# Seven products of matrix quarters instead of eight in part of a two-layer decoder trunk

## Chip, cores and metric

The kernel runs on one core of a Trainium2 chip. The metric is the device time of one execution in microseconds. Five engines work side by side, each through its own list of instructions in order, and wait for each other through semaphores: TensorE (PE in the profile; its loads of stationary operands are listed apart as PEld), VectorE (DVE), ScalarE (ACT), GpSimd (POOL) and SyncE (SP), which here issues the DMAs. SBUF has 128 partitions; TensorE writes into PSUM, whose tiles in this kernel have 512 or 2 x 512 fp32 values in a partition.

## The reference

Two layers on 512 tokens of width 1024, in fp32. Each layer adds a mixer and a SwiGLU feed-forward to the residual, each behind an RMSNorm; a last RMSNorm ends it.

```
h = x
h += sgu(rmsnorm(h, mix_g0));   h += swiglu(rmsnorm(h, ffn_g0))    # layer 0
h += ret(rmsnorm(h, mix_g1));   h += swiglu(rmsnorm(h, ffn_g1))    # layer 1
out = rmsnorm(h, fin_g)

sgu(n):  u, v = split(gelu(n @ w_in));  v = layernorm(v)            # 1024 -> 2 x 1024
         (u * (causal(w_s) @ v + b_s, per chunk of 128)) @ w_out    # 1024 -> 1024
ret(n):  q, k, v, g = split(n @ w_in)    # 4 heads: 256, 256, 512, 512 columns each
         q, k = rotary(q), rotary(k)/16; o = (q k^T * decay) v      # causal
         (rmsnorm(o per head) * gn_g * silu(g)) @ w_out             # 2048 -> 1024
swiglu(n): a, b = split(n @ w_gu);  (silu(a) * b) @ w_down          # hidden 2816
```

Counted in blocks of 1024 rows by 1024 columns of weights the projections are 27.5: `sgu_w_in` 2, `sgu_w_out` 1, two times gate/up 5.5 and down 2.75, `ret_w_in` 6, `ret_w_out` 2.

## The kernel before

Products keep fp32 precision in this way: each operand is split into a high part of the type fp32r and a low part, the rest, and three matmuls are added in PSUM: high by high, high by low, low by high. The weights are split on the chip: a DMA brings a raw tile of 256 rows by 512 columns (`wr`), ScalarE copies it to the high part (`wh`, L112), VectorE subtracts (`wl`, L113); with a gain for each row the lines are L116 and L117. `wr`, `wh` and `wl` have a tag of their own with three buffers each.

`project_t` (L136) makes four tiles of 128 output features by 512 tokens: stationary is a 128 x 128 piece of weights, moving are the 512 tokens of the input, transposed (features on the partitions). `project_n` (L164) makes four tiles of 128 tokens by 512 features: stationary are 128 tokens, moving are the weights. Both walk down the rows of the weights in pairs of 128 (`kp`), and for each of the four output tiles issue 2 x 3 matmuls: L148 to L150, or L159 to L161.

The residual lies transposed in eight tiles `xt`: features on the partitions, tokens along. `residual` (L251) adds the product to it from PSUM, splits the sum with the gain of the next norm into `XH` and `XL` (L238, L239) and adds its square to a running sum. The factor of RMSNorm, `R`, is not needed for the product: `norm_rows` (L208) sums the squares over the partitions with two matmuls against ones and takes the inverse root by three steps of Newton's, and the scaling by `R` is done on the product behind PSUM (L517 and L521 in gate/up, on the rotary tables and on v and g in the heads).

The order: input and its transposition, v in two halves, u in two halves with the mixing between, the gating output `so`; gate/up in eleven groups of 128 + 128 paired columns with silu, product and split behind each; down in two halves of 512 columns with 22 row tiles each; four heads with q and k (256 + 256 columns), v, the scores, g, the score-value product in transposed form, the norm of the head by `norm_rows` and the split of the result `z`; the retention output `ro` in two halves; gate/up again, in whose third and fourth group the residual is transposed back by 32 transposes (`xN`, L670); and down by tokens, its last tile cut in two pieces of 256 columns, so that the end of the kernel is short.

PSUM is held as seven tiles of one bank for products and one for small uses. Most other intermediate tiles (`B`) share one pool of 51. The order on each engine is made when the program is built: a planner walks the instructions by their place in the program as priority, puts each on its engine when its inputs and its tile are there by the planner's own times, and fixes that order; on the chip each engine then goes through its list.

Of the kernel before, what the change touches and what calls it, by code (L numbers as in the profile page):

```python
# [24 lines left out]
WAKE = 5  # L25
EPS = 1e-6
# [17 lines left out]

@with_exitstack
def trunk(ctx, tc, x, positions, mix_g, ffn_g, fin_g, sgu_w_in, sgu_w_s, sgu_b_s, sgu_ln_g, sgu_ln_b,
# [4 lines left out]
    big = ctx.enter_context(tc.tile_pool(name="big", bufs=51))  # L51
    wpool = ctx.enter_context(tc.tile_pool(name="wpool", bufs=3))
    tmp = ctx.enter_context(tc.tile_pool(name="tmp", bufs=6))
    small = ctx.enter_context(tc.tile_pool(name="small", bufs=4))
    psp = ctx.enter_context(tc.tile_pool(name="psp", bufs=7, space=PSUM))
    nps = ctx.enter_context(tc.tile_pool(name="nps", bufs=1, space=PSUM))

    def B(name, dtype=F32R, width=T):
        return big.tile([P, width], dtype, tag="b", name=name)
# [4 lines left out]
    def PS(name):  # L64
        return psp.tile([P, T], F32, tag="ps", name=name)

    def f32(t):
        return t.bitcast(F32)

# [4 lines left out]

    onesr = const.tile([P, P], F32R, name="onesr")
    nc.vector.tensor_copy(onesr, ones)

    nc.scalar.activation(const.tile([P, 1], F32, name="first"), ones[:, 0:1], AF.Gelu_apprx_tanh)
    wake = nps.tile([P, T], F32, tag="nps", name="wake")
    for _ in range(WAKE):  # L80
        nc.tensor.matmul(wake[:, 0:P], ones, ones, start=True, stop=True)
# [12 lines left out]
    def rows_to_cols(name):  # L94
        n = rows_in[name].shape[0]
        ps = nps.tile([P, T], F32, tag="nps", name=f"{name}_ps")
        nc.tensor.transpose(ps[:, 0:n], rows_in[name], ident[0:n, 0:n])
        cols = const.tile([P, n], F32, name=f"{name}_cols")
        nc.vector.tensor_copy(cols, ps[:, 0:n])
        return lambda m: cols[:, m:m + 1]  # L100

    def load_weights(load, name):
        wr = wpool.tile([P, 2, T], F32, tag="wr", name=f"wr_{name}")
        load(wr)
        return wr

    def split_weights(wr, name, cols=None):
        """Rows of the weights, times a gain for each if there is one, as the sum of two F32R parts."""
        wh = wpool.tile([P, 2, T], F32R, tag="wh", name=f"wh_{name}")
        wl = wpool.tile([P, 2, T], F32R, tag="wl", name=f"wl_{name}")  # L110
        if cols is None:
            nc.scalar.activation(wh, wr, AF.Copy)  # L112
            nc.vector.tensor_tensor(wl, wr, f32(wh), ALU.subtract)  # L113
        else:
            for a in range(2):
                nc.scalar.activation(wh[:, a, :], wr[:, a, :], AF.Copy, scale=cols[a])  # L116
                nc.vector.scalar_tensor_tensor(wl[:, a, :], wr[:, a, :], cols[a], f32(wh[:, a, :]), ALU.mult, ALU.subtract)  # L117
        return wh, wl

    def gain_pair(col_of, kp):  # L120
        return None if col_of is None else [col_of(2 * kp + a) for a in range(2)]

    def one_slice(w, c0):
        def load_at(kp):
            src = w[kp * 2 * P:(kp + 1) * 2 * P, c0:c0 + T].rearrange("(a p) n -> p a n", p=P)
            return lambda wr: nc.sync.dma_start(wr, src)
        return load_at

    def two_slices(w, c0, c1):
        def load_at(kp):  # L130
            def load(wr):
                for i, c in enumerate((c0, c1)):
                    src = w[kp * 2 * P:(kp + 1) * 2 * P, c:c + T // 2].rearrange("(a p) n -> p a n", p=P)
                    nc.sync.dma_start(wr[:, :, i * (T // 2):(i + 1) * (T // 2)], src)
            return load
        return load_at  # L136

    def project_t(name, load_at, kt, xh, xl, col_of=None):
        """Four tiles [128 output features, 512 tokens]."""
        ps = [PS(f"ps_{name}_{m}") for m in range(4)]  # L140
        for kp in range(kt // 2):
            n = f"{name}_{kp}"
            wh, wl = split_weights(load_weights(load_at(kp), n), n, gain_pair(col_of, kp))
            for m in range(4):
                for a in range(2):
                    k = 2 * kp + a
                    sl = slice(m * P, (m + 1) * P)
                    nc.tensor.matmul(ps[m], wh[:, a, sl], xh[k], start=(k == 0), stop=False)  # L148
                    nc.tensor.matmul(ps[m], wh[:, a, sl], xl[k], start=False, stop=False)  # L149
                    nc.tensor.matmul(ps[m], wl[:, a, sl], xh[k], start=False, stop=(k == kt - 1))  # L150
        return ps

    def natural_step(ps, c, kp, w, kt, xh, xl, n0=0, n1=T):
        wh, wl = w
        o = ps[:, 0:n1 - n0]
        for a in range(2):
            k = 2 * kp + a
            sl = slice(c * P, (c + 1) * P)
            nc.tensor.matmul(o, xh[k][:, sl], wh[:, a, n0:n1], start=(k == 0), stop=False)  # L159
            nc.tensor.matmul(o, xl[k][:, sl], wh[:, a, n0:n1], start=False, stop=False)  # L160
            nc.tensor.matmul(o, xh[k][:, sl], wl[:, a, n0:n1], start=False, stop=(k == kt - 1))  # L161

    def project_n(name, load_at, kt, xh, xl, col_of=None):
        """Four tiles [128 tokens, 512 output features]."""  # L164
        ps = [PS(f"ps_{name}_{c}") for c in range(NC)]
        for kp in range(kt // 2):
            n = f"{name}_{kp}"
            w = split_weights(load_weights(load_at(kp), n), n, gain_pair(col_of, kp))
            for c in range(NC):
                natural_step(ps[c], c, kp, w, kt, xh, xl)  # L170
        return ps

    def rsqrt_cols(src, n, scale, name):
        """(src * scale + EPS) ** -0.5 of [128, n]."""
        a = small.tile([P, n], F32, tag="ra", name=f"ra_{name}")
        nc.vector.tensor_scalar(a, src, scale, EPS, ALU.mult, ALU.add)
        return rsqrt_of(a, n, name)

    def rsqrt_of(a, n, name):
        i = small.tile([P, n], I32, tag="ri", name=f"ri_{name}")  # L180
        nc.vector.tensor_scalar(i, a.bitcast(I32), 1, None, ALU.logical_shift_right)
        y = small.tile([P, n], F32, tag="ry", name=f"ry_{name}")
        nc.vector.tensor_scalar(y.bitcast(I32), i, -1.0, float(0x5F3759DF), ALU.mult, ALU.add)
        for s in range(3):
# [4 lines left out]
            z = small.tile([P, n], F32, tag="ry", name=f"ry_{name}_{s}")  # L189
# [4 lines left out]
    def rows_of(cols, dst, name):  # L194
        """dst[p, 128 c + t] = cols[t, c] for all p."""
# [4 lines left out]
        ps = nps.tile([P, T], F32, tag="nps", name=f"rp_{name}")  # L200
        for i, part in enumerate((ch, cl)):
# [3 lines left out]
            nc.tensor.matmul(ps, onesr, dg.rearrange("p c t -> p (c t)"), start=(i == 0), stop=(i == 1))  # L205
        nc.vector.tensor_copy(dst, ps)

    def norm_rows(acc, scale, R, name):  # L208
        """R[p, t] = (sum over the partitions of acc[:, t] * scale + EPS) ** -0.5 for all p."""
        h = tmp.tile([P, T], F32R, tag="t", name=f"nh_{name}")  # L210
        nc.scalar.activation(h, acc, AF.Copy)
        l = tmp.tile([P, T], F32R, tag="t", name=f"nl_{name}")
        nc.vector.tensor_tensor(l, acc, f32(h), ALU.subtract)
        ps = nps.tile([P, T], F32, tag="nps", name=f"ns_{name}")
        nc.tensor.matmul(ps, onesr, h, start=True, stop=False)
        nc.tensor.matmul(ps, onesr, l, start=False, stop=True)
        a = TMP(f"na_{name}")
        nc.vector.tensor_scalar(a, ps, scale, EPS, ALU.mult, ALU.add)
        nc.vector.tensor_scalar(R.bitcast(I32), a.bitcast(I32), 1, None, ALU.logical_shift_right)
        nc.vector.tensor_scalar(R.bitcast(I32), R.bitcast(I32), -1.0, float(0x5F3759DF), ALU.mult, ALU.add)  # L220
        t = TMP(f"nt_{name}")
        for _ in range(3):
            nc.vector.tensor_tensor(t, R, R, ALU.mult)
            nc.vector.scalar_tensor_tensor(t, t, -0.5, a, ALU.mult, ALU.mult)
            nc.vector.scalar_tensor_tensor(R, t, 1.5, R, ALU.add, ALU.mult)

    xt = [None] * KD
    XH = xpool.tile([P, KD, T], F32R, name="XH")
    XL = xpool.tile([P, KD, T], F32R, name="XL")
    xh = [XH[:, m, :] for m in range(KD)]  # L230
    xl = [XL[:, m, :] for m in range(KD)]
    acc = [None]

    def R_tile(name):
        return const.tile([P, T], F32, tag="R", name=f"R_{name}", bufs=2)

    def split_x(m, src, col):
        nc.scalar.activation(xh[m], src, AF.Copy, scale=col)  # L238
        nc.vector.scalar_tensor_tensor(xl[m], src, col, f32(xh[m]), ALU.mult, ALU.subtract)  # L239

    def add_square(m, src, name):
        sq = TMP(f"sq_{name}_{m}")
        nc.scalar.activation(sq, src, AF.Square)
        if m == 0:
            acc[0] = sq
        else:
            s = TMP(f"acc_{name}_{m}")
            nc.vector.tensor_tensor(s, acc[0], sq, ALU.add)
# [527 lines left out]
```

## Time and profile before

| | us |
|---|---|
| median of 3 runs (lowest, highest) | 1284.7 (1284.63, 1285.21) |
| span of the profiled execution | 1281.7 |
| busy: TensorE, VectorE, ScalarE | 1269.5, 686.7, 410.7 |

The span reaches from the first to the last instruction of one profiled execution; the time of the runs is that of the whole launch. Busy times of TensorE count overlapped matmuls once. A row of the timeline has the start in us, the duration, the engine, the line, the operation, the tiles (out<-in, numbers left out) and shapes, how many were merged, and in brackets the idle time before it and who ended it. A group row has count, busy time, mean duration in ns, idle time before and what ended it. A row of the waits has who waited for whom, us in total, how often, and the longest.

### The profile page before, as it was taken

The page shows a single profiled execution, that of the slowest core. Times are in us where ns is not written, and L with a number is a line of the kernel's source. Part 1 is how long each engine was busy: PE and PEld are TensorE (multiplying, and loading weights), DVE is VectorE, ACT ScalarE, POOL GpSimd, SP SyncE. Part 2 cuts the span into 40 slices and gives each one's busy share as a digit, 9 for nine tenths or more (in the row PEclk, how much of TensorE's full clock was granted, in tenths as well). Part 3 has the DMA queues.
Part 4 walks back from the last instruction along what each step waited for, and adds up shares of the span by engine and source line. Part 5 has one row for each costly group of instructions (what it writes and reads, how often), then busy time and mean ns, then how long its engine had stood idle before and what let it go on. Part 6 is the DMA issues. An engine that isn't in the chain of part 4 may idle for free.

```text
span 1281.7 us, 14479 instructions
## 1 busy us (share of the span) xinstructions
PE 1269.5 (99%) x5778; PEld 1057.3 (82%) x5778; DVE 686.7 (54%) x962; ACT 410.7 (32%) x548; POOL 16.2 (1%) x23
## 2 busy tenths in 40 slices
PE   8999999999999999999999999999999999999997
PEld 6888888888888888888888888888888888888886
DVE  7575657656453242865848477464474544443323
ACT  5333424323232131332433333223332322322312
POOL 4000000000000000000000000000000000000000
PEclk9999999999999999999999999999999999999999
DMA  4422323333323223322323222222332233323221
GB/s 165 149 82 86 96 91 115 99 99 98 92 93 105 99 99 99 90 91 70 105 81 91 83 87 86 74 91 99 99 98 89 94 99 99 99 96 108 93 99 66
DMA packets 93204, 123.40 MB, mean 96 GB/s; under 512 B 5905, under 2 KB 60241, under 8 KB 93137
## 3 DMA queue, kind: packets, MB, share of 16 engines
q1 hardware_dynamic: 92944, 122.44, 30.1%
q8 instruction: 45, 0.74, 0.2%
q14 instruction: 23, 0.18, 0.0%
q0 software_dynamic: 192, 0.03, 0.0%
HBM read 120.36 MB, written 2.10 MB: 96 GB/s over the span
## 4 chain that ended last, share of the span: by engine, by line
PE 97%; DVE 2%; DMA 1%; SPq 0%; issue 0%; ACT 0%; DVEq 0%
PE ps_gu L148 12%; PE ps_gu L149 12%; PE ps_gu L150 12%; PE ps_dn L148 3%; PE ps_dn L150 3%; PE ps_dn L149 3%; PE ps_dn L160 3%; PE ps_dn L159 3%; PE ps_dn L161 3%; PE ps_qk L148 2%; PE ps_rg L150 2%; PE ps_rg L148 2%; PE ps_qk L150 2%; PE ps_ro L148 2%; PE ps_ro L149 2%; PE ps_rv L159 2%
## 5 line engine op out<-in xcount | busy, mean ns | idle before, releaser
L148 PE MATMUL ps_gu<-XH,wh_gu 128*128 128x512 f32 x704 | 273.9, 389 | 0.2 <-DVE a L517 0.2
L149 PE MATMUL ps_gu<-XL,wh_gu 128*128 128x512 f32 x704 | 273.9, 389 | 0.0
L150 PE MATMUL ps_gu<-XH,wl_gu 128*128 128x512 f32 x704 | 271.6, 389 | 0.0
L113 DVE TENSOR_TENSOR wl_gu<-wr_gu,wh_gu 128x1024 fp32r<-128x1024 f32 x88 | 107.5, 1223 | 176.7 <-ACT wh_gu L112 176.3
L112 ACT ACTIVATE wh_gu<-wr_gu 128x1024 fp32r<-128x1024 f32 x88 | 93.3, 1061 | 236.8 <-PE ps_gu L149 191.5
L148 PEld LDWEIGHTS ps_gu<-XH,wh_gu 128*128 128x128 f32 x704 | 132.1, 188 | 28.1 <-DVE a L517 0.6
L150 PEld LDWEIGHTS ps_gu<-XH,wl_gu 128*128 128x128 f32 x704 | 132.1, 188 | 27.6
L149 PEld LDWEIGHTS ps_gu<-XL,wh_gu 128*128 128x128 f32 x704 | 132.1, 188 | 27.1
L113 DVE TENSOR_TENSOR wl_dn<-wr_dn,wh_dn 128x1024 fp32r<-128x1024 f32 x44 | 53.9, 1225 | 159.2 <-ACT wh_dn L112 159.2
L112 ACT ACTIVATE wh_dn<-wr_dn 128x1024 fp32r<-128x1024 f32 x44 | 46.7, 1061 | 168.9 <-PE ps_dn L160 71.6
L160 PE MATMUL ps_dn<-wh_dn,hl 128*128 128x512 f32 (+1 forms) x198 | 72.5, 366 | 0.0
L159 PE MATMUL ps_dn<-wh_dn,hh 128*128 128x512 f32 (+1 forms) x198 | 72.4, 366 | 0.0
L161 PE MATMUL ps_dn<-wl_dn,hh 128*128 128x512 f32 (+1 forms) x198 | 72.0, 365 | 0.0
L148 PE MATMUL ps_dn<-hh,wh_dn 128*128 128x512 f32 x176 | 68.5, 389 | 0.0
L149 PE MATMUL ps_dn<-hl,wh_dn 128*128 128x512 f32 x176 | 68.5, 389 | 0.0
L150 PE MATMUL ps_dn<-hh,wl_dn 128*128 128x512 f32 x176 | 68.5, 389 | 0.0
L148 PE MATMUL ps_rg<-XH,wh_rg 128*128 128x512 f32 x128 | 50.2, 392 | 0.0
L148 PE MATMUL ps_qk<-XH,wh_qk 128*128 128x512 f32 x128 | 50.1, 392 | 0.0
L148 PE MATMUL ps_ro<-zh,wh_ro 128*128 128x512 f32 x128 | 49.9, 390 | 0.0
L150 PE MATMUL ps_rg<-XH,wl_rg 128*128 128x512 f32 x128 | 49.9, 390 | 0.0
L150 PE MATMUL ps_qk<-XH,wl_qk 128*128 128x512 f32 x128 | 49.9, 389 | 0.0
L150 PE MATMUL ps_ro<-zh,wl_ro 128*128 128x512 f32 x128 | 49.8, 389 | 0.0
(277 smaller groups left out, 2177.8 us busy)
## 6 DMA issues: line engine op xcount, KB each, us to landing
wr_gu<-in_ffn_w_gu SPq DMA_DIRECT2D x176, 256.0 KB, 3.1
wr_dn<-in_ffn_w_down SPq DMA_DIRECT2D x44, 512.0 KB, 3.5
wr_qk<-in_ret_w_in SPq DMA_DIRECT2D x32, 256.0 KB, 3.0
wr_rv<-in_ret_w_in SPq DMA_DIRECT2D x16, 512.0 KB, 3.7
wr_rg<-in_ret_w_in SPq DMA_DIRECT2D x16, 512.0 KB, 3.8
wr_ro<-in_ret_w_out SPq DMA_DIRECT2D x16, 512.0 KB, 3.5
wr_u<-in_sgu_w_in SPq DMA_DIRECT2D x8, 512.0 KB, 3.8
wr_so<-in_sgu_w_out SPq DMA_DIRECT2D x8, 512.0 KB, 3.5
```

The costliest lines, as they stand in the source:

```text
L112: nc.scalar.activation(wh, wr, AF.Copy)
L113: nc.vector.tensor_tensor(wl, wr, f32(wh), ALU.subtract)
L148: nc.tensor.matmul(ps[m], wh[:, a, sl], xh[k], start=(k == 0), stop=False)
L149: nc.tensor.matmul(ps[m], wh[:, a, sl], xl[k], start=False, stop=False)
L150: nc.tensor.matmul(ps[m], wl[:, a, sl], xh[k], start=False, stop=(k == kt - 1))
L159: nc.tensor.matmul(o, xh[k][:, sl], wh[:, a, n0:n1], start=(k == 0), stop=False)
L160: nc.tensor.matmul(o, xl[k][:, sl], wh[:, a, n0:n1], start=False, stop=False)
L161: nc.tensor.matmul(o, xh[k][:, sl], wl[:, a, n0:n1], start=False, stop=(k == kt - 1))
```

## The change

The kernel is written anew around three things.

**Seven products.** In the gating output, both downs, v and g of each head, and the retention output (12.5 of the 27.5 blocks), the product of input and weights is cut into quarters: A by tokens (two halves of 256) and by rows of the weights, B by rows and by columns (two halves of 512). Instead of eight quarter products there are seven, P1, P7, P6, Q4, P5, P2, P3 in this order, of sums of quarters (the scheme of Strassen in Winograd's form). Sums of weights are made on VectorE in the raw tiles (`add`), sums of activations on VectorE as well (`combos`), and each result is split into high and low parts. Chains of products in PSUM are read in between and added to the residual, or, in the heads, copied out and joined there (v is the left half of the columns, g the right).

**Residual by token.** The residual `X` has tokens on the partitions. The norm now acts on X: squares with `accum_out` on ScalarE, the inverse root on VectorE as a chain of small steps (`root`), scaling with gain (`normed`), then eight transposes for each chunk of 128 tokens (`turn`), and the split into `XH` and `XL`. The first gate/up group of each layer and q and k of head 0 run in token halves, tokens 256 to 511 first, so that two chunks can be turned later (`late`). Scores are split for all chunks, the score-value product is made by token, and its result is scaled, gated and transposed (`turn_z`). `norm_rows` and the scaling by R in gate/up and in the heads are gone; the product of silu and b reads PSUM directly, and is not split there but in `combos`.

**Order and memory.** A list of jobs replaces the loops: a job with weights has a fetch (raw DMA), a prep (sums and split) and a run (matmuls); `pipeline` issues fetches up to 6 and preps up to 3 jobs from the current one. Raw weights, both parts, activation parts and most other tiles share one pool `gen` of 22 tiles of 128 x 1024 fp32; six larger tiles hold inputs before they are split, five tiles of 512 are for short use. PSUM is four tiles of two banks. The feed-forward's hidden 22 row tiles are taken in pieces of 8, 8 and 6: down of a piece follows after gate/up groups 6, 9 and 11, so gate/up and down alternate.

```diff
+def pipeline(jobs):
+    weighted = [i for i, j in enumerate(jobs) if j.prep is not None]
+    f = p = 0
+    done = 0
+    for i, job in enumerate(jobs):
+        while f < len(weighted) and f < done + FETCH:
+            jobs[weighted[f]].fetch()
+            f += 1
+        while p < len(weighted) and p < done + PREP:
+            jobs[weighted[p]].prep()
+            p += 1
+        if job.prep is not None:
+            done += 1
+        job.run()
...
-    big = ctx.enter_context(tc.tile_pool(name="big", bufs=51))
-    wpool = ctx.enter_context(tc.tile_pool(name="wpool", bufs=3))
+    gen = ctx.enter_context(tc.tile_pool(name="gen", bufs=N_GEN))
...
+    PRODUCTS = ("P1", "P7", "P6", "Q4", "P5", "P2", "P3")
+
+    def seven(name, w, r0, np_, c1, c2, A, evac, mid=None):
...
+        def prep(p, s, nk):
+            use = {"P1": "b11", "P7": "t", "P6": "t", "Q4": "t", "P5": "b12", "P2": "b21", "P3": "b22"}[p]
+            extra = {"P7": "b12", "P6": "b11", "Q4": "b21", "P5": "b11"}.get(p)
+            if extra:
+                add(use, extra, s, nk)
+            parts[p, s] = split(raw[use, s], f"{name}_{p}_{s}", nk)
+
+        chain = {"P1": "X", "P7": "Y", "P6": "X", "Q4": "Y", "P5": "X", "P2": "Z", "P3": "X"}
...
+    def combos(name, raw, np_):
...
+            elif p == "P7":
+                summed("S3", quarter(0, 0), quarter(1, 0), ALU.subtract)
+                src = sums["S3"]
+            elif p == "P6":
+                summed("S1", quarter(1, 0), quarter(1, 1), ALU.subtract)
+                summed("S2", sums["S1"], quarter(0, 0), ALU.subtract)
+                src = sums["S2"]
...
+            h, l = new(f"{p}h", F32R), new(f"{p}l", F32R)
+            if sign == 1.0:
+                nc.scalar.activation(h, src, AF.Copy)
+                nc.vector.tensor_tensor(l, src, f32(h), ALU.subtract)
...
+    def into_x(part):
...
+        def evac(p, acc, c):
+            if p == "P1":
+                plus(xq(0, 0), acc["X"], ALU.add)
...
+    def normed(name, g, more=None):
...
+            xs = G(f"xs_{name}_{c}", F32, (P, D))
+            nc.vector.scalar_tensor_tensor(xs, X[:, c, :], r, gt[0], ALU.mult, ALU.mult)
+
+            def turn_late():
+                ps = turn(c, xs, name)
...
+            late.append(turn_late)
...
+            def evac(ps):
+                if extra is not None:
+                    extra(j)
+                sl = G(f"silu{l}_{j}")
+                nc.scalar.activation(sl, ps[0], AF.Silu)
...
+        for j in range(6):
+            group(j)
+        down(0)
+        for j in range(6, 9):
+            group(j)
+        down(1)
+        for j in range(9, 11):
+            group(j)
+        down(2)
```

1022 lines of the change are left out of this document (564 added, 458 removed).

## The prediction

> **What bounds the kernel now.** I read the page first, then the busy time of each engine by stage, then TensorE's waits, and last single rows of the timeline for prices.
>
> ```profile
> span 1281.7 us, 14479 instructions
> PE 1269.5 (99%) x5778; PEld 1057.3 (82%) x5778; DVE 686.7 (54%) x962; ACT 410.7 (32%) x548; POOL 16.2 (1%) x23
> PE rp_n L205 <- DVE dg_n L203: 1.8, 1, 1.8
> PE wake L81 <- POOL ones L73: 1.2, 1, 1.2
> PE ps_v L159 <- ACT wh_v L116: 1.1, 1, 1.1
> PE xT L284 <- DMA xn<-in_x: 1.0, 1, 1.0
> PE ps_gu L148 <- DVE a L517: 0.2, 1, 0.2
> ```
>
> The last five lines are all of TensorE's waits: 5.3 us in the whole run. So TensorE's instruction stream is the time, and VectorE, busy for 54%, costs nothing yet. By stage (columns: PE, PEld, DVE, ACT, POOL busy, clock):
>
> ```profile
> 112.90:156.50 43.60, 43.60 (x195) 36.12 (x194) 27.01 (x37) 18.77 (x26) 0.00 (x0) 1.00 0.30 97
> 156.50:396.80 240.30, 240.14 (x1059) 198.50 (x1058) 137.69 (x189) 75.14 (x93) 0.00 (x0) 1.00 0.32 98
> 396.80:516.50 119.70, 119.70 (x530) 99.11 (x529) 40.34 (x44) 32.05 (x37) 0.00 (x0) 1.00 0.30 99
> 516.50:823.00 306.50, 306.50 (x1426) 257.84 (x1424) 201.56 (x289) 106.59 (x144) 0.00 (x0) 1.00 0.29 87
> 823.00:910.60 87.60, 87.60 (x388) 72.50 (x388) 43.40 (x55) 26.53 (x33) 0.00 (x0) 1.00 0.28 90
> 1274.70:1281.70 7.00, 0.15 (x2) 0.00 (x0) 2.21 (x9) 1.53 (x4) 0.00 (x0) 0.83 0.40 150
> ```
>
> These are the gating output, gate/up, down, the four heads, the retention output and the tail. TensorE is full in each. Down (third line) is the stage to look at: VectorE has 40 us of work in 120 us there, and it is where the change puts most of its new VectorE work.
>
> **Prices.** The stretch from start to start on a full engine is what a step costs.
>
> ```profile
> 300.25 0.39 PE L148 MATMUL ps_gu<-XH,wh_gu 128*128 128x512 f32 x1
> 300.93 0.39 PE L148 MATMUL ps_gu<-XH,wh_gu 128*128 128x512 f32 x1
> 976.38 1.91 PE L670 MATMUL xN<-ident,xt 128*128 128x128 f32 x16
> 978.04 0.48 PE L148 MATMUL ps_gu<-XH,wh_gu 128*128 128x512 f32 x1
> 1274.09 0.28 PE L160 MATMUL ps_dn<-wh_dn,hl 128*128 128x256 f32 x1
> 1274.21 0.28 PE L161 MATMUL ps_dn<-wl_dn,hh 128*128 128x256 f32 x1
> 605.58 1.23 DVE L113 TENSOR_TENSOR wl_rv<-wr_rv,wh_rv 128x1024 fp32r<-128x1024 f32 x1
> 606.72 0.68 DVE L223 TENSOR_TENSOR nt_o<-RO 128x512 f32<-128x512 f32 x1
> 612.16 2.49 DVE L650 TENSOR_TENSOR z<-y,RO 128x512 f32<-128x512 f32 x4
> 614.57 0.68 DVE L552 TENSOR_TENSOR rotq<-ps_qk,cosR 128x512 f32<-128x512 f32 x1
> 63.72 0.17 DVE L176 TENSOR_SCALAR ra_ln<-mv 128x4 f32<-128x4 f32 x1
> 65.91 0.16 DVE L190 SCALAR_TENSOR_TENSOR ry_ln<-ru_ln,ry_ln 128x4 f32<-128x4 f32 x1
> L112 ACT ACTIVATE wh_gu<-wr_gu 128x1024 fp32r<-128x1024 f32 x88 | 93.3, 1061 | 236.8 <-PE ps_gu L149 191.5 <-issue 22.4 <-PE ps_ro L149 8.8
> ```
>
> A 512-wide matmul: 0.68/3 = 0.227 us. A transpose: 1.66/16 = 0.104. A 256-wide matmul: 0.12. VectorE, two operands: 1.14 for 1,024 elements, 0.60 for 512 (2.41/4), also out of PSUM (the L552 row lasts 0.68 like L223). A chain of small steps: 12 in 2.4 us, 0.20 each. ScalarE's copy: 1.06.
>
> **TensorE's own sum.** A projection block is 1024 rows by 1024 outputs for 512 tokens: 8 x 8 x 3 x 512-wide, 192 matmuls. With seven products 168. 12.5 blocks lose 24 each: 300 x 0.227 = -68.1 us. Three groups (first gate/up of each layer, first query/key) run in token halves, 192 x 0.12 instead of 96 x 0.227: +1.3 each, +3.8; the 132 narrow matmuls of the last down become wide, -0.9. Transposes: three norms by token need 32 each and the heads' outputs 64, while 32 for the last residual go: +128 x 0.104 = +13.3. The 14 matmuls that summed squares over partitions go, -3.2. Scores and score-value products change shape; from the same rates about +1 and -1.6, together -0.6. Sum: **-55.7 us**. More loads of weights (the third quarter is fetched twice) I cost at nothing: the DMA share is 0.3 in all stages.
>
> **VectorE's sum where the seven products are.** For one 512-row by 512-column set of quarters (np_=4), VectorE does 14 low parts of weights (8 before, since each quarter was split once), 8 weight sums, 7 low parts and 4 sums of the activations, and 7 additions into X: 40 steps of 1,024 elements, 40 x 1.14 = 45.6 us, against 168 x 0.227 = 38.1 for TensorE. The last down piece (np_=3) has 7 x 1.74 + 4 x 1.74 + 11 x 0.87 + 7 x 1.14 = 36.7 against 126 x 0.227 = 28.6. So these stages turn from a third of VectorE's time to more than all of it. ScalarE has 21 copies, 22 us: not the bound. What VectorE can do ahead decides: weights are prepared two jobs beyond the running one (PREP), in gate/up VectorE is idle for more than half and gets lighter (no scaling by R, no split of h).
>
> How far ahead it gets I read from the allocation of tiles. In the kernel before, results of the rotation come from one pool in the order of the program, and a later one waits for an earlier one's issue though its inputs are there:
>
> ```profile
> 619.91 0.68 DVE L555 TENSOR_TENSOR rotq<-ps_qk,cosR 128x512 f32<-128x512 f32 x1
> 623.53 1.23 DVE L113 TENSOR_TENSOR wl_rv<-wr_rv,wh_rv 128x1024 fp32r<-128x1024 f32 x1 [1.14 <-ACT wh_rv L112]
> 625.87 0.68 DVE L562 TENSOR_TENSOR rlq<-rrq,rhq 128x512 fp32r<-128x512 f32 x1
> 626.47 0.68 DVE L559 TENSOR_TENSOR rrq<-rotq,rotq 128x512 f32<-128x512 f32 x1
> ```
>
> The second rrq needs only rotq, done by 620.6; VectorE even stood still for 1.14 us, but it comes right behind rlq, the allocation before it. After the change raw weights, their parts, activations' parts, silu and rotated q and k all come from one pool of 22 tiles. So in-place sums and additions into X can run ahead, but nothing that needs a tile.
>
> Stalls of TensorE, each with its ends (0 if all is done ahead):
> - Down, np_=4, four times. No lead at all: 45.6 - 38.1 = 7.5. Ahead lie the first three weight splits, four or five in-place sums and half the first activation split, some 8.5 steps; but up to P5's first job VectorE has 24 steps against 27 us of TensorE and their chains through ScalarE (1.06 each) leave gaps. I take 4 each: 16.
> - Down, np_=3, twice: 8.1 to 0; the second activation half comes only from the group just before. 5.5 each: 11.
> - Gating output: 7.5 plus the gate's 8 x 0.60; I take 4.5.
> - Heads: rotation is serial through the pool (two times 1.14 + 1.14 + 1.2 + 1.06 + 1.14 = 5.7, of which the first may start 2.7 early), then P7's second weight; it is due 8.2 after P1 begins and ready near 10, with the hand-overs between engines near 10.7. 2.5 each (0 to 5.8): 10.
> - Retention output, twice: VectorE is over its time, with a head's values beside it. 4 each (0 to 9): 8.
> - The three norms. In the kernel before, the scaling by R came after the product, with three spare PSUM tiles, and cost TensorE nothing. Now the product needs the normalised, transposed input. From the end of P5: two additions 1.2, square about 0.8, 13 small steps 2.6, then scale (1.2) chunk by chunk; P3's weights wait behind these tiles, ready near 8.5 where P2 covers 5.4: 3. At the other end the transpose of the last chunk sits after the last half-group, so its 1.06 + 1.14 are bare: 2.5. About 6, and 7.5 before the heads (P2 is shorter at np_=3); 0 to 12 each: 19.5.
> - Start and tail: +2; the tail is again addition, square, small steps, scale and store, 7 us.
>
> Sum 71. The profiled execution is 1281.7, 3.0 below the median of the runs, 1284.7, and I add the change to the median: 1284.7 - 55.7 + 71 = **1300 us**, slower by 1.2%. With no stall at all 1229; with all upper ends 30 + 16.2 + 12.3 + 23.2 + 18 + 36 + 2 = 138, 1367.
>
> **Rivals.**
> 1. *VectorE gets ahead* (faster). Place: the six down pieces and the norms. If the pool's order costs little and the idle VectorE of gate/up (137.7 of 240.3 now, less after) takes a whole product's worth ahead, downs and outputs stall 1 each, norms 3, heads 1: 8 + 9 + 4 + 2 = 23, and 1284.7 - 55.7 + 23 = 1252. It decides once stalls stay under 55.7. For it: P1, P7, P2 come in an order that leaves each addition into X a whole product of time, so only sums over a block matter. Against: 45.6 to 38.1, and the order of allocation above. A third: 0.33.
> 2. *Stalls slow TensorE itself* (slower still). The first matmuls ran at half the pace of the later ones:
>
> ```profile
> 10.04 0.43 PE ps_v L161
> 10.46 0.43 PE ps_v L159
> ```
>
> 0.43 against 0.227, at a time when TensorE had just waited for data. Here some 20 stalls of 2 to 6 us would come; if half of them are followed by 3.5 us at that pace, each costs 1.7 more, 17 us, and longer gaps with them: near 1335. Against: the stalls break up into short waits at single jobs. 0.12.
> [...]
> 3. *Gain and stalls cancel*: stalls of 53 to 58, 1284.7 within 0.2% (about 2.6 us, what a measurement here can tell from no change): 0.05.
>
> **Chances.** Mine, 1300 with its own range of 1288 to 1320, has 0.5; rivals 0.33, 0.12, 0.05. So faster 0.33, same 0.05, slower 0.62. The range for 8 in 10 runs from rival 1's 1252, less a little, to rival 2: 1250 to 1338.
>
> **What would show it.** Right: TensorE's busy time falls to about 1215 and its waits on VectorE (wl, the activation parts, XL) rise from 5 to some 70 us; VectorE's busy share in the down pieces is over 0.95, and in gate/up under 0.35; each np_=4 piece lasts about 42 us instead of 38.1, a norm leaves TensorE idle for some 6 us, a head lasts about 75 us (76.6 now: 306.5/4). If waits are under 40, rival 1 holds; if matmuls of 0.43 or a granted clock under 0.95 appear behind gaps, rival 2. The prediction is wrong at its root if VectorE is not the releaser of TensorE's waits, for instance if loads held by the common pool are.

## The result, and the profile after

The kernel after takes 1346.26 us (median of 4 runs, 1344.86 to 1349.88) beside 1284.95 before: a ratio of 1.0482, 95% interval 1.0466 to 1.0498, 61.3 us slower. Its profiled execution has a span of 1345.7 us, 64.0 more. From its page: the span, the busy time of the engines, the granted clock in 40 slices (9 is nine tenths or more) and what the DMAs moved.

```profile
span 1345.7 us, 14802 instructions
PE 1258.9 (94%) x5766; PEld 1039.6 (77%) x5766; DVE 892.5 (66%) x1148; ACT 505.3 (38%) x642; POOL 4.1 (0%) x12
PEclk9999989999999999899999999998999999999998
DMA packets 106965, 151.19 MB, mean 112 GB/s; under 512 B 6760, under 2 KB 61072, under 8 KB 106896
```

TensorE's busy time fell by 10.6 us only, but a matmul that runs at half pace counts as busy (a 512-wide row at a clock of 0.50 lasts 0.63 instead of 0.39, in the last timeline of this section). So I took all of TensorE's rows, from start to start, and split each step into the price of its shape (0.227, 0.12, ...) and the excess over it: a wait where the engine stood still, half pace where it did not. (The second name is somewhat too wide: of its 38.4 us below, 25 lie in stretches whose granted clock is 0.50; the rest are steps that lasted longer at full clock.) By price TensorE's work went from 1263.3 to 1208.3, -55.0. The excess went from 12.8 (waits 5.2, half pace 7.6) to 123.9 (85.6 and 38.4). From the last matmul's end to the end of the span it was 6.8 and is 12.1. Those three, -55.0 + 111.1 + 5.3 = 61.4, leave 2.6 of the 64.0 to excesses below 0.06 us a step and to rounding.

By stage (columns as before: PE, PEld, DVE, ACT, POOL busy, clock, DMA share, GB/s): the gating output and the norm behind it, a long down piece, the gate/up groups that follow it, the last down piece of layer 0 with its norm and the first q and k, the first half of the retention output, the tail.

```profile
115.00:164.00 49.00, 42.59 (x178) 33.43 (x177) 45.57 (x55) 24.64 (x33) 0.00 (x0) 0.93 0.48 150
308.00:352.00 44.00, 41.40 (x176) 32.36 (x175) 43.50 (x38) 24.13 (x24) 0.00 (x0) 1.00 0.55 180
352.00:416.00 64.00, 64.00 (x284) 52.97 (x284) 19.81 (x18) 11.72 (x12) 0.00 (x0) 1.00 0.24 74
503.00:580.00 77.00, 64.69 (x359) 56.37 (x358) 68.29 (x102) 36.54 (x55) 0.00 (x0) 0.91 0.35 110
849.00:923.00 74.00, 58.37 (x243) 47.07 (x242) 65.82 (x82) 29.97 (x40) 0.00 (x0) 0.86 0.30 100
1333.50:1345.70 12.20, 0.10 (x1) 0.00 (x0) 7.91 (x32) 0.72 (x2) 0.00 (x0) 0.71 0.41 155
```

In the long down piece VectorE is busy for 43.50 of 44 us, in gate/up for 19.81 of 64: the work is where the prediction put it. The waits of TensorE, largest first, and two of ScalarE's (total, times, longest):

```profile
PE zT L924 <- DVE sg L915: 12.3, 2, 7.2
PE Y_dn L181 <- ACT wh_dn_Q L159: 7.0, 6, 1.4
PE xT_f L488 <- DVE xs_f L502: 5.9, 3, 2.4
PE X_dn L181 <- ACT wh_dn_P L159: 5.4, 5, 3.6
PE ps_qk L181 <- ACT wh_qk L159: 5.1, 4, 4.4
ACT wh_dn_P L159 <- DVE wr_dn_t L274: 30.4, 10, 3.4
ACT wh_dn_Q L159 <- DVE wr_dn_t L274: 27.7, 10, 4.2
```

Of TensorE's, only the first has single waits of more than 5 us. Where ScalarE's copies (`wh`) are named for the downs, ScalarE itself is busy for 24.13 us of the 44: as its own two rows show, it waits for the sums that VectorE makes in the raw tiles. And behind short waits TensorE ran slow, here in a long down piece of layer 1 (columns: start, duration, then the idle time before in brackets):

```profile
1225.51 0.39 PE L181 MATMUL X_dn<-wh_dn_P,h_P6h 128*128 128x512 f32 x1
1227.29 0.47 PE L181 MATMUL Y_dn<-wh_dn_Q,h_Q4h 128*128 128x512 f32 x1 [1.39 <-ACT wh_dn_Q L159]
1228.33 0.50 PE L182 MATMUL X_dn<-wl_dn_P,h_P6h 128*128 128x512 f32 x1 [0.57 <-DVE wl_dn_P L160]
1228.67 0.39 PE L183 MATMUL X_dn<-wh_dn_P,h_P6l 128*128 128x512 f32 x1
...
1230.13 0.63 PE L182 MATMUL X_dn<-wl_dn_P,h_P6h 128*128 128x512 f32 x1
1230.55 0.63 PE L183 MATMUL X_dn<-wh_dn_P,h_P6l 128*128 128x512 f32 x1
```

From 1230.13 to 1230.55 is 0.42, not 0.227, after waits of 1.39 and 0.57. The last section shows when the clock halved and when it did not.

### The profile page after: what moved, and what is told of

Its sections match the earlier page's. It is cut to its first block, busy times and chain, and to the rows that moved or that the text cites. A ratio compares the mean times of both kernels' runs of the same rounds, so it can differ in the third digit from the quotient of the medians.

```text
span 1345.7 us, 14802 instructions
## 1 busy us (share of the span) xinstructions
PE 1258.9 (94%) x5766; PEld 1039.6 (77%) x5766; DVE 892.5 (66%) x1148; ACT 505.3 (38%) x642; POOL 4.1 (0%) x12
## 5 line engine op out<-in xcount | busy, mean ns | idle before, releaser
L181 PE MATMUL ps_gu<-XH,wh_gu 128*128 128x512 f32 (+1 forms) x768 | 286.0, 373 | 4.1 <-ACT wh_gu L159 4.1
L182 PE MATMUL ps_gu<-XL,wh_gu 128*128 128x512 f32 (+1 forms) x768 | 286.3, 373 | 3.2 <-DVE XL L491 3.2
L183 PE MATMUL ps_gu<-XH,wl_gu 128*128 128x512 f32 (+1 forms) x768 | 285.7, 374 | 0.0
L181 PE MATMUL ps_qk<-XH,wh_qk 128*128 128x512 f32 (+1 forms) x160 | 57.1, 357 | 5.4 <-ACT wh_qk L159 5.1
L182 PE MATMUL ps_qk<-XL,wh_qk 128*128 128x512 f32 (+1 forms) x160 | 56.4, 353 | 0.0
L183 PE MATMUL ps_qk<-XH,wl_qk 128*128 128x512 f32 (+1 forms) x160 | 56.2, 353 | 0.0
L160 DVE TENSOR_TENSOR wl_dn_P<-wr_dn_b,wh_dn_P 128x1024 fp32r<-128x1024 f32 (+1 forms) x48 | 53.1, 1131 | 0.0
L159 ACT ACTIVATE wh_dn_P<-wr_dn_b 128x1024 fp32r<-128x1024 f32 (+1 forms) x48 | 45.1, 978 | 4.4 <-DVE wl_dn_P L160 1.6
L160 DVE TENSOR_TENSOR wl_vg_P<-wr_vg_b,wh_vg_P 128x1024 fp32r<-128x1024 f32 x32 | 38.3, 1222 | 11.8 <-ACT wh_vg_P L159 11.7
L274 DVE TENSOR_TENSOR wr_dn_t<-wr_dn_t,wr_dn_b 128x1024 f32<-128x1024 f32 (+1 forms) x36 | 40.5, 1131 | 0.0
L181 PEld LDWEIGHTS ps_qk<-XH,wh_qk 128*128 128x128 f32 x160 | 31.2, 195 | 11.0 <-ACT wh_qk L159 6.6
```

Source lines behind the costliest of these rows:

```text
L159: nc.scalar.activation(h, s, AF.Copy)
L160: nc.vector.tensor_tensor(l, s, f32(h), ALU.subtract)
L181: nc.tensor.matmul(o, ah, bh, start=start, stop=False, skip_group_check=True)
L182: nc.tensor.matmul(o, ah, bl, start=False, stop=False, skip_group_check=True)
L183: nc.tensor.matmul(o, al, bh, start=False, stop=stop, skip_group_check=True)
L274: nc.vector.tensor_tensor(d, d, o, ALU.add)
```

## The experiments

Times are compared with the kernel before (1284.4 to 1285.0 in each set of runs) and with the 1346.3 of the change. The edits are shortened: `...` stands for what is left out.

**What the two halves of the change cost.** Eight products everywhere, in the new order and with the residual by token:

```diff
-            seven(f"vg{hd}", ...); seven(f"dn{l}_{s}", ...); seven("so", ...); seven(f"ro{j}", ...)
+            project_n(f"v{hd}", ...); project_n(f"g{hd}", ...); eight(...) for so, downs and ro
```

> Eight products everywhere, so that only the new order, the residual by token and the common pool are left of the change (v and g of a head now as in the kernel before, all tokens by a tile of weights). TensorE gets back 4 x 24 x 4 x 0.227 less 4 x 24 x 3 x 0.227, that is 21.8 us over the run with eight in the outputs and downs (1323.1). Theory 'the rebuilding costs by itself what the seven products then cannot give back': 1323.1 + 21.8 less the some 10 us of stalls that the seven products cause in the heads, 1330 to 1345, so 45 to 60 above the kernel before, and nearly all of the change's loss is the rebuilding. Theory 'the seven products' VectorE work is the loss, and the rebuilding is about free': within 10 us of the 1284.7 of before.

1335.4 (ratio 1.0401, 1.0384 to 1.0419). The rebuilding alone costs 50.7 us; the seven products as they were put add 10.8. By the same split of TensorE's rows as above: 13.1 more work (transposes, token halves), 31.2 more waits and half pace, 6.8 more tail.

(`eight` takes all tokens by a tile of weights and adds the result to X by column halves.) Eight only in the gating output, the downs and the retention output; seven stay in the heads:

> Eight products instead of seven in the gating output, both downs and the retention output, all else as in the changed kernel (residual by token, heads with seven). TensorE's work grows by 204 matmuls of 0.227, 46 us. If VectorE's load in those stages makes the waits, nearly all of them go there (about 5 + 21.7 + 20 + 20 us with the stretches at half clock) and the run ends near 1325, faster than the changed kernel: seven products are then the cause of the loss. If the residual by token and the rest of the new structure make it, and the seven products pay, the run gets longer by 30 to 46 us, to 1375 to 1392.

1323.1 (1.0298, 1.0268 to 1.0328). Seven products in the heads alone are thus worth 12.3 of the 21.8 us that they take off TensorE; in the other places they lose 23.

**VectorE's load.** Without the weight sums:

```diff
-            if extra:
-                add(use, extra, s, nk)
```

> The changed kernel without the sums of weights (the add in prep is left out, all loads stay), so the weights of P7, P6, Q4 and P5 are wrong ones. If VectorE's amount of work sets the time of the seven-product stages: 8 of 40 steps of 1.14 us go from each np_=4 piece, 36.5 us of VectorE for 38.1 of TensorE; the four np_=4 down pieces fall from 43.5 to 44.8 us to about 40, and the whole run by 25 to 35 us, to some 1315, with fewer stretches at half clock. If the order of allocation in the common pool is what holds TensorE, the sums (in place, without a tile) matter little: less than 10 us.

1314.2 (1.0229, 1.0199 to 1.0258), 32 less, as VectorE's load would have it. But this run also takes the sums out of the chain that ScalarE's copies wait for (the wait of TensorE for `wh_dn_Q`, 7.0 us above, is gone), so it does not tell load and chain apart. The same sums moved to GpSimd:

```diff
-            nc.vector.tensor_tensor(d, d, o, ALU.add)
+            nc.gpsimd.tensor_tensor(d, d, o, ALU.add)
```

> All weight sums move from VectorE to GpSimd: the 8 sums of a long block, 9.1 us of its 45.6 of VectorE work, leave VectorE. Theory 'VectorE is the bound in these blocks': if GpSimd keeps up and hinders nobody, about the 1314 of the run without the sums. Theory 'the two engines share something': in the kernel before, small VectorE steps lasted several times as long while GpSimd added tiles near the start; then each of VectorE's steps beside a sum is stretched, and the time is 1346 or more. GpSimd's own pace also counts: if a sum takes it more than about 38/8 = 4.7 us, it becomes the bound itself.

1382.5 (1.0760, 1.0736 to 1.0783). VectorE's and GpSimd's rows of one down piece in that run:

```profile
318.76 1.22 DVE L341 TENSOR_TENSOR h_S<-h_S,h 128x1024 f32<-128x1024 f32 x1
319.90 3.40 DVE L160 TENSOR_TENSOR wl_dn_P<-wr_dn_t,wh_dn_P 128x1024 fp32r<-128x1024 f32 x1
323.23 1.21 DVE L368 TENSOR_TENSOR h_Q4l<-h,h_Q4h 128x1024 fp32r<-128x1024 f32 x1
324.36 1.21 DVE L384 TENSOR_TENSOR X<-X,Y_dn 128x1024 f32<-128x1024 f32 x1
...
318.93 3.29 POOL L274 TENSOR_TENSOR wr_dn_t<-wr_dn_t,wr_dn_b 128x1024 f32<-128x1024 f32 x1 [21.85 <-DVE wl_dn_P L160]
323.38 3.31 POOL L274 TENSOR_TENSOR wr_dn_t<-wr_dn_t,wr_dn_b 128x1024 f32<-128x1024 f32 x1 [1.16 <-DVE wl_dn_P L160]
```

A step that took 1.22 takes 3.40 where it runs beside a sum of 3.29, and ends 1.1 us after the sum does: VectorE gains nothing here, nor in the whole run (busy 899.0 us beside 892.5 in the changed kernel). The addition out of PSUM at 324.36 keeps its 1.21 beside the next sum. The means over the run agree: 20 steps `wl_dn_P<-wr_dn_t,wh_dn_P` last 1.98 us and 16 steps `wl_vg_P<-wr_vg_t,wh_vg_P` 2.16, where both last 1.22 in the changed kernel; 20 additions `X<-X,X_dn` out of PSUM last 1.21, there 1.22.

**Order, pool and waits.** The activation parts of P1, P7 and P6 of the four long down pieces asked for one gate/up job earlier:

```diff
+            project_t(f"gu{l}_{j}", ..., mid={2: early[j]} if j in early else None)
```

> The activation parts of P1, P7 and P6 of the first two down pieces of each layer are asked for inside the last gate/up group ahead of them, before its silu takes a tile. VectorE's work stays the same, but some 9 steps lie where VectorE idles. If the order of allocation is what keeps VectorE from working ahead: each of the four np_=4 down pieces loses 3 to 4.5 of its 4.4 to 5.8 us of waits and half pace, 12 to 18 us in all, about 1330. If the mere sum of work binds inside the piece, or tiles run out, less than 5 us.

1327.2 (1.0330, 1.0300 to 1.0360), 19 less. None of the four pieces has an excess left, and a window inside one has TensorE full; VectorE's work is the same in all (893.9 us beside 892.5), but part of it now lies ahead of the piece:

```profile
305.00:343.00 38.00, 38.00 (x170) 31.46 (x169) 35.54 (x32) 21.31 (x21) 0.00 (x0) 1.00 0.53 180
```

So here it was the place in the order, not the sum of 45.6 us by itself, that made TensorE wait. (The place decides both when a step gets its tile and where it stands in its engine's list; the run does not tell these apart.) Two more tiles in the pool do nothing:

```diff
-N_GEN = 22
+N_GEN = 24
```

> The changed kernel with 24 tiles in the common pool instead of 22 (the most that fits). Theory 'the pool is full: parts are late because loads and parts hold its tiles': two tiles more are one weight tile with its parts further ahead, worth a job's 4.5 us at most of the 17 seven-product pieces, and a time of 1335 or less. Theory 'order and VectorE's work decide, not the number of tiles': 1343 to 1347.

1346.7 (1.0482, 1.0467 to 1.0498). Head 3's values straight after the head, and its turn one product later:

```diff
-            if hd < 3:
-                then(values)
+            then(values)
```

> The values of head 3 are made right behind its v and g, as for the other heads, and turned at P6 of the first retention output; before, values stood at P7 and the turn at P2. In the changed kernel TensorE waits 12.3 us for sg ahead of the transposes there, and 21 of the 73 us from 849 to 922 are waits and half pace. If that is a matter of the place in the order, these waits go: 12 to 18 us less in all, about 1330. If VectorE simply has too much to do in the two output products, the wait moves to another tile and the run gets less than 5 us shorter.

1339.9 (1.0429): 6 less, between the two. The wait of 12.3 is gone from the list, but others take half of its place (one of 2.9 for `wh_ro_P` is new). Matmuls without use where TensorE waits:

```diff
+                    for _ in range(44):
+                        nc.tensor.matmul(ps[:, 0, 0:P], onesr, onesr, start=True, stop=True)
```

> The changed kernel with matmuls that compute nothing used (18 of 512 columns, at 0.227 us 4.1 us, ahead of the late turns of each feed-forward norm; 44 of 128 columns ahead of each half of head 3's turn), placed where TensorE waits longest. Theory 'TensorE's pace halves because it has waited': the waits there are filled, the half-pace rows right behind them go, and the time falls by 5 to 8 us although TensorE has more to do. Theory 'the half pace comes at fixed times whatever TensorE did': half-pace time stays near 31 us and the time stays within 3 us of 1346 or grows by what the added matmuls last beyond the waits.

1346.3 (1.0468, 1.0451 to 1.0486): the second theory's time, but not its clock. (The 18 matmuls ahead of a late turn have 128 columns too, not 512; at 0.11 each in the trace they last 2.0 us, not 4.1.) Its row for the first half of the retention output, to be read beside the one above:

```profile
849.00:923.00 74.00, 70.15 (x352) 59.10 (x353) 70.87 (x87) 33.46 (x43) 0.00 (x0) 0.98 0.30 100
```

The clock there is 0.98 instead of 0.86, so the half pace there did come from the waits; but the added matmuls last as long as what they replace: over the run, by the split into price and excess, 13 us more work for 9 less waits and 6 less half pace.

**Putting it together.** Seven products only where the runs so far let them pay (four long downs with early parts, heads) and, untried alone, in the first half of the retention output; eight elsewhere; with them, several changes of order:

```diff
-                seven(f"dn{l}_{s}", ...)          # s == 2, as well as so and ro1
+                eight(f"dn{l}_{s}", ...)
-    output(0, {"P7": heads[3][3], "P2": heads[3][2]})
+    output(0, {"P6": heads[3][2]})                # values straight after the head
```

> This puts together what the runs so far point to: eight products in the gating output, in the last down piece of each layer and in the second half of the retention output (the places whose end a norm follows, or whose activation halves come late); seven in the four long down pieces, with the activation parts of P1, P7 and P6 asked for one job earlier in the group before; seven in the first half of the retention output and in the heads, with the values of head 3 straight after the head; P3's parts of head 0's input asked for at P5 instead of before the scores; the first chunk turned ahead of the gains' transposes. Theory 'the cost is local: the order of allocation at the four long down pieces, VectorE's sums at the pieces before a norm': from 1323.1 (eight in all these places) less 4 x 24 x 2 x 0.227 = 43.6 us of matmuls would be 1280 if nothing stalled; less 4 x 24 x 0.227 = 21.8 for the four long pieces and 5.4 for the first half of the retention output, and some 15 for head 0, head 3 and the start: 1276 to 1290. Theory 'total VectorE load': seven products in five pieces bring back stalls of 4 to 5 us each, 1305 or more.

1306.3 (1.0170, 1.0154 to 1.0185): the second theory's number, but not at its places. The four long pieces have no excess at all; the first half of the retention output has 11 us, each norm 7 to 12. With eight in that half as well:

```diff
-            seven("ro0", ...)
+            eight("ro0", ...)
-N_GEN = 22
+N_GEN = 24
```

> The hybrid once more, with eight products in the first half of the retention output too and 24 tiles in the pool: seven only in the four long down pieces and in v and g of the heads. The 11 us of waits and half pace of that half go for 5.4 us of matmuls: 1306.3 - 5.7 = 1300 if the pool's size means nothing, 1290 to 1297 if it does. It ends above the kernel before in either case, if the norms (about 10 us each of waits and half pace at the three of them) and the tail are what is left.

1299.6 (1.0122, 1.0103 to 1.0142). Against all eight, 1335.4, this is 36 less, where 8 x 24 x 0.227 = 43.6 us of matmuls are gone. The changes of order around head 3, head 0 and the start are in it too, so the share of the seven products is an estimate: 12.3 in the heads and 21.8 in the long pieces, which have no excess, make 34. What is left is mostly the rebuilding. Its waits before and behind the norms were the next suspect:

```diff
-                if kp < np_ - 2:
+                if kp < np_ - 3:
...
-                            plus(0, c, c + 1)
-                            part(0, 1, (c,))
+                    plus(0, 0, 2)
+                    part(0, 1, (0, 1))
...
-                if kp >= 2:
-                    then(late_one)
+                if kp == 1:
+                    then(late_one)
+                    then(late_one)
```

and, in the tail, a square root on ScalarE with one step of Newton's, as in the kernel before.

> The second hybrid (1299.6) with only the order around the norms, head 0 and the tail changed: at the end of a projection that a norm follows, three pairs of rows of each token chunk are kept back instead of two, so that the last two chunks cover 8.2 us of the root's chain instead of 5.4; those two chunks get one root together instead of two, and are added to the residual together; both late turns come after the second row pair of the group in token halves, not after the third and the fourth; head 0's scores come one product later; at the end of the kernel the root is taken by ScalarE's square root, a reciprocal and one step, the left half is multiplied by the gain ahead of time, and ScalarE scales it. Theory 'the rebuilding costs by waits at its few serial places': its 4.8 us of waits before each norm's first matmul shrink to 2 (three places), the 9 and 5 us at the late turns of the feed-forward norms to 2 each, head 0's 5 to 2, the tail's 13.6 to 8: 27 less, 1270 to 1280, below the kernel before. Theory 'VectorE is short of time there whatever the order': less than 10 us less, 1290 or more.

1285.05 (1.0003, 0.9994 to 1.0012), level with the kernel before, 14.5 less than without; 5 short of the forecast. The tail shrank from 13.6 to 10.3, the late turns no longer wait; head 0 did not gain (5.1 us of wait for `k0h`). With two pairs kept back (`kp < np_ - 2` again, the rest as it is):

> The same with two pairs of rows kept back, as in the kernel as changed. If the three pairs' weight parts, which stay in the common pool longer, crowd out the next group's parts, this one is the faster; if the cover of the root's chain is what counts, it is 5 to 8 us slower than its neighbour (three places, 2.7 us each).

1292.0 (1.0055, 1.0038 to 1.0072): 6.9 slower, so the cover counts. With four (`kp < np_ - 4`):

> As the run with the norms reordered (1285.05), with all four pairs of rows of each token chunk kept back instead of three where a projection has four (gating output and second half of the retention output; the last down pieces have three and keep all back already). What is left there are 3.7 and 3.5 us of waits between the last transposes and the first matmul of gate/up, and 2.7 and 1.7 us of half pace behind them. Theory 'order': the transposes fall among the last chunk's matmuls, both places lose most of it: 8 us less, 1276 to 1280, faster than before by 0.4 to 0.7%. Theory 'the pool': four weight tiles' parts, eight tiles of 24, crowd out the next group's parts: the same time or longer, 1284 or more.

1286.1 (1.0016, 1.0007 to 1.0025): nothing. Four pairs and v and g of head 0 in eight products:

```diff
+            if hd == 0:
+                project_n("v0", ...); scores; project_n("g0", ...)
+            else:
                 seven(f"vg{hd}", ...)
```

> The run with four pairs kept back, and v and g of head 0 in eight products (24 more matmuls, +5.4 us), the sums of the input's quarters made during head 0 for the others. VectorE has no idle time from the first late turn to head 0's scores in the run with the norms reordered, and TensorE waits 5.3 us there for k's high part and runs some 11 matmuls at half pace (2.4). Theory 'VectorE's load at that place': these 7.7 us go, 2 us less than its neighbour. Theory 'the chain of the rotation itself is late': the wait stays, 4 to 5 us more than its neighbour.

**1281.45** (0.9976, 0.9968 to 0.9985), 4.6 less than its neighbour in spite of 5.4 us more of matmuls. The wait for `k0h` is gone, so the chain of the rotation was not too long by itself; VectorE's load in head 0 is the likely cause, but the edit also moves the scores and the parts of the input, and load and place are not told apart. This is faster than both kernels, though by only 0.24% (2.9 us) against the one before. What is left at a norm, in its timeline:

```profile
158.11 0.39 PE L183 MATMUL ps_so<-wh_so,so_l 128*128 128x512 f32 x1
158.34 1.91 PE L557 MATMUL xT_f<-ident,xs_f 128*128 128x128 f32 x16
162.62 0.50 PE L181 MATMUL ps_gu<-XH,wh_gu 128*128 128x256 f32 x2 [2.37 <-ACT XH L559]
```

The transposes stand behind all matmuls of the projection, and the split behind them is bare. With the scaled input in other tiles and the transposes asked for earlier:

```diff
-            xs = G(f"xs_{name}_{c}", F32, (P, D))
+            xs = RAW(f"xs_{name}_{c}")...          # for the two feed-forward norms
...
+                            if c == 1 and k2 == np_ - 2:
+                                late_one()
+                                late_one()
                             mm(c, k2)
```

> The run with head 0 in eight products (1281.45), with the scaled input of the two feed-forward norms in the larger tiles instead of the common pool, and the transposes of the first two chunks asked for ahead of the last two pairs of rows of the last chunk. Theory 'pool and place': the transposes run among the last matmuls, 3.5 us of waits and some 2 of half pace go at both places: 8 to 11 us less, 1271 to 1274. Theory 'the chain itself is too long': the waits move ahead of the transposes, 1280 to 1283.

1285.5 (1.0003, 0.9994 to 1.0012), a miss to the other side: the input was scaled by 155.6 but the transposes still began at 158.4, and the wait grew to 3.8. The growth has a plain cause: in ScalarE's list a copy of weights, which waited for its load, now stands ahead of the split of the transposes (`XH`, at 159.42 in the run before and at 162.16 here):

```profile
161.20 1.06 ACT L159 ACTIVATE wh_gu<-wr_gu 128x1024 fp32r<-128x1024 f32 x1 [2.21 <-DMA wr_gu<-in_ffn_w_gu]
162.16 1.92 ACT L559 ACTIVATE XH<-xT_f 128x1024 fp32r<-128x1024 f32 x2
```

The place of the transposes among the matmuls is set by TensorE's fixed list, and I have not found how to move them; that stays open.

## Why the prediction was wrong

The side was right, the size not: 1300 with 1250 to 1338 forecast, 1346 measured. TensorE's work came out as forecast; the whole miss lies in the stalls, 119 us against 71. Of these 48 us, 31 are half pace, which the sum had at nothing; 11 are waits (80.4 against 69), nearly all in the retention output; 6 are the start and the tail.

| step of the prediction | forecast | measured |
|---|---|---|
| TensorE's own sum | -55.7 | -55.0 |
| down, np_=4, four times | 16 | 21.7 |
| gating output and first norm | 10.5 | 19.4 |
| down, np_=3, twice, and norm before the heads | 18.5 | 27.4 |
| heads | 10 | 11.7 |
| retention output and its norm | 14 | 31.3 |
| start and tail | 2 | 7.6 |
| stalls together | 71 | 119 |

(Measured: excess of the stage's rows over their price, less the same before; the 5.3 of the tail and the 2.6 that no stage holds are in the last line but one. The split by stages is good to about 1 us, by how the smallest steps are priced.)

- **TensorE's own sum** was right to 0.7 us, and so was the cause of most stalls: VectorE at 0.99 in the down pieces, 0.31 in the gate/up behind them, its sums behind the waits. What it had named as signs held there too (a piece of np_=4 lasts 43.5 to 44.8 us to the gate/up group behind it, 42 said); TensorE's busy time fell to 1258.9 and not to 1215, since half pace counts as busy.
- **Rival 2, half pace**, had 0.12 and a price of 17. It happened: 31 of the 119 us (38.4 - 7.6), of which some 24 at a clock of 0.50, in 68 us of such stretches. The 3.5 us of it that the price put behind a stall no run had shown in mid-run: the kernel before has it, ahead of the tail, at the start alone (clock 0.51 from 9.60 to 13.02 us). What came were stretches of 3.41 us, up to five in a row. The step that failed is "the stalls break up into short waits at single jobs". They did: single waits above 3.41 us were four, of 3.6 to 7.2. But half clock began at thirteen places, ten of them without such a wait, one of them behind waits of 1.39 and 0.57 close together; not every stall had it behind it (last section). I had priced it only on top of stalls of 71, as another case, when in this run it came with the stalls themselves. At the measured 30.8 of half pace to 80.4 of waits, the 69 us of stalls in my sum would have come to 95, and the forecast to 1326: better, but 20 short, because the waits themselves were too small at the places below.
- **"Retention output, twice: 4 each"** failed at the first half: 21.2 of the 31.3 (waits 16.6, half pace 4.6). The prediction had "a head's values beside it" but no row for them: 12 small steps that each wait for the one before stand between steps of 1.22, and the turn, which is in TensorE's list ahead of the next products, waits for the last.

```profile
908.57 0.16 DVE L433 SCALAR_TENSOR_TENSOR ru_o<-rt_o,ra_o 128x2 f32<-128x2 f32 x1
908.64 1.22 DVE L341 TENSOR_TENSOR z_S<-z,z 128x1024 f32<-128x1024 f32 x1
909.78 0.15 DVE L435 SCALAR_TENSOR_TENSOR ry_o<-ru_o,ry_o 128x2 f32<-128x2 f32 x1
909.90 1.22 DVE L341 TENSOR_TENSOR z_S<-z_S,z 128x1024 f32<-128x1024 f32 x1
...
914.18 0.47 PE L924 MATMUL zT<-ident,sg 128*128 128x128 f32 x1 [7.19 <-DVE sg L915]
```

- **The norms** were put at 6, 6 and 7.5. Half pace behind them and the late turns' own waits were left out; order and shorter chains there and in the tail got 14.5 us back. **The tail** was said to be "7 us again": it is 12.1, since two roots of 13 steps follow each other.
- **"VectorE's sum" as the bound of a down piece** was half right. Without the sums 32 us go; but with the same work and the first parts asked for one job earlier the piece runs full. The second half of the step, that the order decides what runs ahead, is what held; whether through the pool's tiles or the engines' lists is open.
- **Split by the two halves of the change**: the forecast had -68.1 + 49.5 = -18.6 for the seven products and about 34 for the rebuilding (12.4 of work on TensorE, 19.5 at the norms, 2). Measured are +10.8 and 50.7: the seven products, forecast as a gain, were a loss as they were put. That the side of the whole came out right rests on the rebuilding, which was forecast to lose and lost more. Rival 1, which would have needed stalls under 55.7, is out for this order of work. It is nearly what the four long pieces do once their parts are asked for early.

## What to carry to other kernels

Work taken off a full engine is worth what is left after the stalls at the place where the replacing work must be done, so price each such place alone: its own load on the other engine, what that engine can start ahead by its place in the order, and the chain of small steps that ends in it. Add up the waits that fall close together, too: where they came to 1.73 us or more within one stretch of 3.41 us in the clock record here, the next stretch ran at a clock of 0.50. When a change is a loss, measure its halves apart before mending: here the rebuilding, not the seven products, was four fifths of it, and the seven products pay where their sums have an idle VectorE ahead.

## What the hardware showed that I had not expected

In the changed kernel the granted clock halved mostly where no single wait was long: at ten of its thirteen places none came to 3.41 us. In the clock record, the stretches at half clock before the tail, the first at 126.91 us, all begin at whole multiples of 3.41 us from each other and last 3.41 us or a multiple of it (once, twice and five times), 68 us in all. The four long down pieces wait alike (TensorE is idle for 2.60 to 2.62 us of each), but lie differently on this grid. Here are neighbouring stretches of the first piece (three rows) and of the last (two rows; columns as in the stages above):

```profile
321.47:324.89 3.42, 2.57 (x12) 1.79 (x10) 3.42 (x4) 1.73 (x2) 0.00 (x0) 1.00 0.45 154
324.89:328.30 3.41, 2.32 (x9) 1.75 (x10) 3.41 (x4) 1.34 (x2) 0.00 (x0) 1.00 0.42 153
328.30:331.71 3.41, 3.41 (x17) 2.67 (x15) 3.41 (x4) 1.88 (x2) 0.00 (x0) 1.00 0.43 124
1226.01:1229.42 3.41, 1.56 (x6) 1.12 (x7) 3.41 (x5) 2.00 (x2) 0.00 (x0) 1.00 0.51 166
1229.42:1232.83 3.41, 3.41 (x10) 2.64 (x9) 2.60 (x3) 1.11 (x2) 0.00 (x0) 0.50 0.00 0
```

In the first piece TensorE is idle for 0.85 and 1.09 us of two stretches, the clock stays at 1.00, and the piece lasts 43.5 us. In the other three, 1.73 to 1.91 us of idle time fall into one stretch, the next is at 0.50, and they last 44.7 to 44.8. From 20 us to the tail, all thirteen stretches at full clock with 1.73 us of idle time or more were followed by one at 0.50, and none of those with 1.64 or less. So in this trace it was the idle time summed within a stretch, not the single wait, that told the two kinds apart: single waits of 1.39 us were part of stretches followed by half clock, and one of 1.97 (for `wh_v`), 1.06 of it in one stretch and 0.91 in the next, was followed by full clock.

And in the run with the sums on GpSimd, a step of VectorE on two inputs from SBUF lasted 3.40 us beside a sum instead of 1.22, while one with an input from PSUM kept its 1.21.
